# A decoder layer with expert retrieval: one more top-k in the dense stage, gate rows by a matmul with ones, one-hots shared with VectorE

## The chip, the cores and the metric

One NeuronCore of a Trainium2 chip runs the whole kernel. Its engines are TensorE (PE in the rows), VectorE (DVE), ScalarE (ACT), GpSimd (POOL) and SyncE (SP, which here only issues transfers). The metric is the time on the device in microseconds, the median of three runs. A second measurement, one profiled execution, gives the rows below.

## The reference, cut to what matters

One layer on 1024 tokens of width 1024. Six modulation rows come from the condition c: two shifts, two scales, two gates. After the mixing part (a gMLP half and an S5 state space half, joined by an output projection with gate gt1), a PEER block retrieves for each token and each of 8 heads the 16 best of 16,384 experts, and adds their weighted sum with gate gt2.

```python
cond = jax.nn.silu(c)
mod = cond @ w_ada[l] + b_ada[l]
sh1, sc1, gt1, sh2, sc2, gt2 = jnp.split(mod[:, None, :], N_MOD, axis=-1)
h = _rmsnorm(x, g_mix[l]) * (1.0 + sc1) + sh1
z = h @ w_in[l]                     # gMLP u, gMLP v, S5 input
y = jnp.concatenate([y_gm, y_ssm], axis=-1) @ w_out[l]
x = x + gt1 * y
h2 = _rmsnorm(x, g_ffn[l]) * (1.0 + sc2) + sh2
x = x + gt2 * _peer(h2, w_q[l], peer_keys[l], peer_u[l], peer_v[l])
return _rmsnorm(x, g_final)

# _peer, for a block t of 128 tokens
s = jnp.einsum('thcd,hckd->thck', q, keys)
top_s, top_i = lax.top_k(s, PEER_TOPK)
best_s, pos = lax.top_k(cand_s, PEER_TOPK)      # of all 16 x 16 sums
g = jax.nn.softmax(best_s, axis=-1)
act = jax.nn.gelu(jnp.einsum('thkd,td->thk', u_tab[idx], t))
return jnp.einsum('thk,thkd->td', g * act, v_tab[idx])
```

## The kernel before

The 1024 tokens are eight blocks of 128. A dense stage does the mixing part for all blocks, in two halves of four, and then for each block b an output projection (outproj, tiles po, with the gate row bc), a score (score, item sb: transposes ptf, queries pq, scores psc on TensorE) and a top-k on VectorE (route, item r, in 28 steps; tiles m, ixs, scr, mk).

The experts of blocks 0 to 4 are then computed for all 16,384 experts in 128 tiles of 128, weighted by a matrix G that is zero where an expert wasn't chosen. G is built by scatter (item s): for each of a token's 128 choices one-hot rows are compared out (hot and a on VectorE), scaled by the weight (b, on VectorE for every dv[block]-th pair of choices and on ScalarE for the rest), and multiplied on TensorE (pgs), copied out (GS) and written to HBM (G_d). An expert tile i has stage1 (pa: 192 matmuls with u, in three products of split values), a weighing (w, wh, wl), and per four tiles a stage2 (res and pd, with v). u and v of a tile are split by ScalarE and VectorE after their load. Five lead tiles go first, as the item ld.

The experts of blocks 5 to 7 are fetched row by row with indirect transfers from GpSimd: per block 128 rows of u (ru, multiplied on VectorE, summed on ScalarE), then 128 rows of v (rv, accumulated into gacc on VectorE). This is the generator side_work. It first does the top-k of the blocks from NDB + early on, here block 7 alone, then releases the score's buffers, then fetches; the loop over expert tiles pulls per steps of it for each tile, 6.3 here. Each block's end is finish: scale by gt2, add, normalise (msf, rf), scale by g_final, write.

The order of the dense stage is written by a table, CFG["plan"]: each item has a start and a duration, and needs other items; its steps are sorted by these times and become the program. A scheduler then orders each engine's instructions from there. So a changed entry moves whole items on all engines.

The modulation parts enter in two forms. As columns (mod_late): the sum of the weighted rows of w_ada, mc, is made on VectorE and summed over partitions by eight matmuls of 128 x 1 (pm), and b_ada is added on VectorE. The two gates are wanted as rows on all partitions: row_bcast makes eight diagonal tiles (diag) on VectorE and multiplies each by ones (pb_gt1, pb_gt2), then ScalarE copies the result (bc). gate1 does this for gt1, late_gt2 for gt2, which is written to HBM (gt2_d). mod5 makes mc5 from eight row blocks of w_ada, two in each load (wada5), with two buffers.

Of the kernel before, what the change touches and what calls it, by code (L numbers as in the profile page):

```python
# [41 lines left out]
CFG = dict(xo=[2, 3, 4, 0, 1], gt=3, ss=7, hs=2, b1=6, nw=6, raw=1, ngb=3, rows=4, lead=5, per=6.3, dv=[6, 9, 9, 2, 99], early=2,  # L42
# [6 lines left out]
    gt=(858.2, 122), rel=(739, 334), s4=(981.8, 131.5), r5=(916.4, 58.6), r6=(989.9, 124.6), ld=(776, 675.7),  # L49
# [6 lines left out]
    wo1=(-962.7, 7.3), so=(-926.7, 23.4), vn=(-891, 2.4), g1=(-703.9, 14.2), ax=(-882.1, 8.1), m3=(-856.1, 38.5),  # L56
# [41 lines left out]
def tile_hybrid_layer(ctx: ExitStack, tc: tile.TileContext, a, out, cfg=CFG):  # L98
# [27 lines left out]
    def bankB(name):  # L126
        return psB.tile([P, 2, 512], F32, tag="b", name=name)
# [83 lines left out]
    def mod_sums(i):  # L211
        mp = bankB(f"mp{i}").rearrange("p a b -> p (a b)")
        k = 0
        for w, n in early[i]:
            for kk in range(n):
                if k:
                    V.scalar_tensor_tensor(mp, w[:, kk], cs[:, k:k + 1], mp, op0=ALU.mult, op1=ALU.add)
                else:
                    V.tensor_scalar(mp, w[:, kk], cs[:, k:k + 1], None, op0=ALU.mult)
                k += 1  # L220
            yield
        mc = sm.tile([P, D], F32, tag="x", name=f"mc{i}", bufs=3)
        A.copy(mc, mp)
        mod_late(i, mc)

    def mod_load(i, src):
        ws, k = [], 0
        for c in src:
            n = {"X": 4, "p": 2, "x": 1}[c]
            v = a["w_ada"][k * P:(k + n) * P, i * D:(i + 1) * D].rearrange("(k p) n -> p k n", p=P)  # L230
            if c == "X":
                w = sB.tile([P, 4, D], F32, tag="X", name=f"wada{i}_{k}", bufs=1)
            elif c == "x":
                w = sm.tile([P, 1, D], F32, tag="x", name=f"wada{i}_{k}", bufs=3)
# [815 lines left out]
    def mod5():  # L1050
        mc = sm.tile([P, D], F32, tag="x", name="mc5", bufs=3)
        for k in range(0, KD, 2):
# [19 lines left out]
    def prep_steps(n):  # L1072
# [13 lines left out]
        au=(lambda: z_u(0, wzu[0]), 4, "wu"), ax=(lambda: mix(0), 2, "au vn"), g1=(gate1, 1, "m2"),  # L1086
# [3 lines left out]
        gt=(gt2_row, 1, "m5"), rel=(release, NDB, "gt op7 sb7"), ld=(lambda: lead(0, L), 2 * L, "rel"))  # L1090
# [402 lines left out]
```

## Time and profile before

| | us |
|---|---|
| median of three runs | 2656.88 (2655.66 to 2659.79) |
| the profiled execution | 2655.86 |
| its span | 2653.9 |
| dense stage up to the first tile after the five lead tiles | about 918 |
| expert tiles 5 to 127 | to about 2600 |

In the rows a matmul's count x is of passes: a float32 matmul is two of them. A bracket at the end of a row is the engine's idle time before it, with the line of what ended it. The granted clock is 1.00 at 2.4 GHz. VectorE is busy 85% of the span, ScalarE 49%, GpSimd 44%.

### The profile page before, as it was taken

The numbers are of one execution on the slowest core, as the hardware profiler recorded it, in microseconds if no ns is written. First come the engines' busy times: TensorE is split into PE (matmuls) and PEld (weight loads), VectorE is DVE, ScalarE is ACT, GpSimd is POOL, SyncE is SP. The second block draws the span as 40 slices with busy tenths as digits, with TensorE's granted clock in tenths as the row PEclk, the third lists the DMA queues.
The fourth block names the chain that finished last, engine by engine and source line by source line (L and its number), as shares of the span: only waits on it lengthen the run. The fifth ranks groups of instructions, "written<-read, shape, count | busy, mean of one in ns | idle before, by whom it ended". The sixth has DMA issues, their size and how long they took to land. (4 is left out here: it accounts for less than half of the span.)

```text
span 2653.9 us, 39049 instructions
## 1 busy us (share of the span) xinstructions
PE 2538.1 (96%) x14119; PEld 2168.1 (82%) x14119; DVE 2267.8 (85%) x4215; ACT 1312.8 (49%) x2315; POOL 1180.9 (44%) x842
## 2 busy tenths in 40 slices
PE   6999999999877999999999999999999999999997
PEld 2548677678666898989999989999999988999986
DVE  7984699869899888789989888889999888899898
ACT  2311246568868377773222577762223767732222
POOL 0001000000000177676667578766665767776660
PEclk9996999999988999999999999999999999999999
DMA  9546233444636699999999999899998999999993
GB/s 362 108 121 217 101 122 104 126 136 135 181 118 193 218 328 326 343 327 364 341 340 375 325 336 330 331 354 364 341 355 326 334 345 343 325 368 345 343 365 139
DMA packets 301761, 726.85 MB, mean 274 GB/s; under 512 B 42448, under 2 KB 133072, under 8 KB 301152
## 3 DMA queue, kind: packets, MB, share of 16 engines
q0 software_dynamic: 112832, 411.09, 42.4%
q1 hardware_dynamic: 165600, 254.48, 28.6%
q10 hardware_dynamic: 23136, 58.79, 6.2%
q8 instruction: 111, 1.82, 0.3%
q14 instruction: 82, 0.67, 0.1%
HBM read 660.70 MB, written 62.39 MB: 272 GB/s over the span
## 5 line engine op out<-in xcount | busy, mean ns | idle before, releaser
L888 POOL DMA_INDIRECT ru<-in_peer_u_dram,ix x384 | 637.7, 1661 | 897.6 <-issue 745.1
L959 PE MATMUL pa<-Th,u 128*128 128x320 f32 x4096 | 911.3, 310 | 4.9 <-DVE u L936 3.1
L959 PEld LDWEIGHTS pa<-Th,u 128*128 128x128 f32 x4096 | 688.4, 188 | 8.7 <-DVE u L936 3.6
L888 POOL DMA_INDIRECT rv<-in_peer_v_dram,ix x384 | 522.8, 1361 | 257.4 <-DVE gacc L916 168.0
L959 PE MATMUL pa<-Tl,u 128*128 128x320 f32 x2048 | 633.4, 309 | 0.0
L899 DVE TENSOR_TENSOR ru<-ru,hn 128x2048 f32<-128x2048 f32 x192 | 438.6, 2289 | 113.1 <-DMA ru<-in_peer_u_dram,ix 106.6
L894 ACT ACTIVATE jk<-ru 128x1024 bf16<-128x1024 f32 x384 | 405.4, 1056 | 213.2 <-issue 167.7
L916 DVE SCALAR_TENSOR_TENSOR gacc<-rv,act,gacc 128x1024 f32<-128x1024 f32 x381 | 489.2, 1284 | 6.4 <-DVE u L936 0.4
L1006 PE MATMUL pd<-v,wh 128*128 128x512 f32 x1280 | 402.6, 390 | 3.2 <-ACT wh L980 1.6
L997 PE MATMUL res<-v,wh 128*128 128x512 f32 x1280 | 400.7, 390 | 0.8 <-ACT wh L980 0.8
L959 PEld LDWEIGHTS pa<-Tl,u 128*128 128x128 f32 x2048 | 385.3, 188 | 1.7
L1006 PEld LDWEIGHTS pd<-v,wh 128*128 128x128 f32 x1280 | 238.8, 188 | 52.5 <-ACT wh L980 2.5
L997 PEld LDWEIGHTS res<-v,wh 128*128 128x128 f32 x1280 | 239.6, 188 | 50.4 <-ACT wh L980 1.6
L961 ACT ACTIVATE w<-pa 128x320 f32<-128x320 f32 x256 | 108.7, 431 | 333.7 <-PE pa L959 311.9
L698 ACT ACTIVATE b<-hot,gT 128x128 f32<-128x128 f16 x520 | 233.5, 537 | 61.0 <-PE pgs L700 36.0
L1006 PE MATMUL pd<-v,wl 128*128 128x512 f32 x640 | 248.7, 390 | 1.7 <-DVE wl L982 1.6
L997 PE MATMUL res<-v,wl 128*128 128x512 f32 x640 | 248.1, 389 | 1.3 <-DVE wl L982 1.3
L935 ACT CAST u<-ur 128x1024 fp32r<-128x1024 f32 x128 | 133.5, 1043 | 205.3 <-DMA ur<-in_peer_ut_dram 79.0
L700 PE MATMUL pgs<-a,b 128*128 128x128 f32 x1280 | 188.9, 299 | 46.2 <-DVE a L690 19.3
L700 PEld LDWEIGHTS pgs<-a,b 128*128 128x128 f32 x1280 | 169.9, 207 | 68.4 <-ACT b L698 35.3
L936 DVE TENSOR_TENSOR u<-ur,u 128x1024 fp32r<-128x1024 f32 x128 | 156.3, 1221 | 29.7 <-ACT u L935 23.2
L943 ACT CAST v<-vr 128x1024 fp32r<-128x1024 f32 x128 | 133.7, 1045 | 94.1 <-DMA vr<-in_peer_v_dram 76.8
(349 smaller groups left out, 3050.4 us busy)
## 6 DMA issues: line engine op xcount, KB each, us to landing
vr<-in_peer_v_dram SPq DMA_DIRECT2D x128, 512.0 KB
ur<-in_peer_ut_dram SPq DMA_DIRECT2D x128, 512.0 KB
G_d<-GS SPq DMA_DIRECT2D x40, 1024.0 KB
Gt<-G_d ACTq DMA_DIRECT2D x64, 640.0 KB
wada<-in_w_ada_dram SPq DMA_DIRECT2D x17, 1024.0 KB
wo<-in_w_out_dram SPq DMA_DIRECT2D x8, 1024.0 KB
ru<-in_peer_u_dram,ix POOLq DMA_INDIRECT x384
rv<-in_peer_v_dram,ix POOLq DMA_INDIRECT x384
```

The source lines that it names most:

```text
L698: A.activation(b1[:, n], hot[:, :, o + n], AF.Copy, scale=gT[:, s1 + o + n:s1 + o + n + 1])
L700: T.matmul(pg[:, o // 4, (o % 4) * P:(o % 4 + 1) * P], b1[:, o % 2], a1[:, o % 4], start=True, stop=True)
L888: G.indirect_dma_start(out=row[:, e], out_offset=None, in_=a[src], in_offset=bass.IndirectOffsetOnAxis(ap=ix[:, s0 + e:s0 + e + 1], axis=0))
L894: A.activation(junk, row[:, e], AF.Copy, accum_out=act[:, s + e:s + e + 1])
L899: V.tensor_mul(row, row, bcast(hn, 1, GP))
L916: V.scalar_tensor_tensor(ac, row[:, e], w, ac, op0=ALU.mult, op1=ALU.add)
L935: A.copy(u[:, 0], ur)
L936: V.tensor_tensor(u[:, 1], ur, u[:, 0].bitcast(F32), op=ALU.subtract)
L943: A.copy(v[:, 0], vr)
L959: T.matmul(pa[:, :NN], l[:, k, :], r[:, k, ns], start=(k == 0 and m == 0), stop=(k == KD - 1 and m == 2))
L997: T.matmul(res[tb][n], l[:, ts], r[:, n * 512:(n + 1) * 512], start=(g == 0 and q == 0 and m == 0), stop=(g == NGR - 1 and q == QG - 1 and ...
L1006: T.matmul(po, l[:, ts], r[:, n * 512:(n + 1) * 512], start=(q == 0 and m == 0), stop=(q == QG - 1 and m == 2))
```

## The change

Some numbers of the table and a new helper:

- early goes from 2 to 1: block 6's top-k leaves the plan (item r6) and is done in side_work, ahead of block 7's. per goes from 6.3 to 6.6.
- dv of block 4 goes from 99 to 2: half of its b pairs are made on VectorE, where ScalarE made all but one.
- The items rel and ld get shorter durations (rel 60 instead of 334, ld 150 instead of 675.7), and rel needs m5 instead of gt.
- gate_row takes the place of row_bcast and mod_late for the mods 2 and 5: a row of b_ada (br, 1024 elements, reordered in the transfer) is loaded by SyncE, and four matmuls of 512 columns with ones sum mc over partitions and add br into a row on all partitions (pb), which ScalarE copies. gt1 is made in mod_sums(2), gt2 in mod5; items g1 and gt are gone.

```diff
-CFG = dict(..., per=6.3, dv=[6, 9, 9, 2, 99], early=2,
+CFG = dict(..., per=6.6, dv=[6, 9, 9, 2, 2], early=1,
...
-    gt=(858.2, 122), rel=(739, 334), s4=(981.8, 131.5), r5=(916.4, 58.6), r6=(989.9, 124.6), ld=(776, 675.7),
+    rel=(739, 60), s4=(981.8, 131.5), r5=(916.4, 58.6), ld=(776, 150),
...
         mc = sm.tile([P, D], F32, tag="x", name=f"mc{i}", bufs=3)
         A.copy(mc, mp)
-        mod_late(i, mc)
+        if i == 2:
+            gt1 = sm.tile([P, D], F32, name="bc1", bufs=1)
+            gate_row(i, mc, gt1)
+        else:
+            mod_late(i, mc)
...
+    def gate_row(i, mc, dst):
+        br = sm.tile([P, D], F32, tag="x", name=f"br{i}", bufs=3)
+        nc.sync.dma_start(br[:1].rearrange("o (k p) -> o k p", p=P), a["b_ada"][:, i * KD:(i + 1) * KD].rearrange("p (o k) -> o k p", o=1))
+        pb = bankB(f"pb{i}")
+        for n in range(2):
+            for r, p in ((mc, P), (br, 1)):
+                T.matmul(pb[:, n], ones[:p], r[:p, n * 512:(n + 1) * 512], start=(p == P), stop=(p == 1))
+        A.copy(dst, pb.rearrange("p a b -> p (a b)"))
...
-    def row_bcast(dst, col, name):
-        pb = bankB(f"pb_{name}")
-        for k in range(KD):
-            dg = sm.tile([P, P], F32, tag="diag", name=f"diag_{name}{k}", bufs=2)
-            V.tensor_scalar(dg, ident, col[:, k:k + 1], None, op0=ALU.mult)
-            T.matmul(pb[:, k // 4, (k % 4) * P:(k % 4 + 1) * P], ones, dg, start=True, stop=True)
-        A.copy(dst, pb.rearrange("p a b -> p (a b)"))
-        return dst
...
             if k == KD - 2:
-                mod_late(5, mc)
-            yield
-
-    def gt2_row():
-        late_gt2()
-        yield
+                bc2 = sm.tile([P, D], F32, tag="x", name="bc2", bufs=3)
+                gate_row(5, mc, bc2)
+                nc.scalar.dma_start(gt2_d, bc2)
+            yield
...
-        gt=(gt2_row, 1, "m5"), rel=(release, NDB, "gt op7 sb7"), ld=(lambda: lead(0, L), 2 * L, "rel"))
+        rel=(release, NDB, "m5 op7 sb7"), ld=(lambda: lead(0, L), 2 * L, "rel"))
```

TensorE's order around pzu of the first half, the matmuls that stand ahead of py (pzv and pzu are gMLP projections), before:

```order
L491 MATMUL pzv0_3_1100<-wzv_0_305,hT0_0_129 128x512 x4
L491 MATMUL pzv0_3_1100<-wzv_1_306,hT0_1_130 128x512 x4
L248 MATMUL pm2_1113<-ones_80,mc2_1111 128x1 x8
L536 MATMUL pzu0_0_1464<-hT0_0_129,wzu_0_1123 128x512 x4
L536 MATMUL pzu0_0_1464<-hT0_1_130,wzu_1_1124 128x512 x4
```

and now:

```order
L505 MATMUL pzv0_3_1100<-wzv_0_305,hT0_0_129 128x512 x4
L505 MATMUL pzv0_3_1100<-wzv_1_306,hT0_1_130 128x512 x4
L256 MATMUL pb2_1116<-mc2_1111,ones_80 128x512
L256 MATMUL pb2_1116<-br2_1114,ones_80 128x512
L256 MATMUL pb2_1116<-mc2_1111,ones_80 128x512
L256 MATMUL pb2_1116<-br2_1114,ones_80 128x512
L550 MATMUL pzu0_0_1463<-hT0_0_129,wzu_0_1122 128x512 x4
L550 MATMUL pzu0_0_1463<-hT0_1_130,wzu_1_1123 128x512 x4
```

The eight matmuls pm2 of one column give way to four of 512 columns, pb2, at the same place.

TensorE's order from the GLU matmuls pg of the first half to the first score (ptf0), before; po0 and po1 are output projections of blocks 0 and 1, pb_gt1 a piece of gate row 1, pm5 the columns of mod 5:

```order
L637 MATMUL po0_1916<-wo2_1814,ss0_1823 128x512 x4
L637 MATMUL po0_1916<-wo3_1812,ss0_1823 128x512 x4
L557 MATMUL pb_gt1_1857<-diag_gt17_1879,ones_80 128x128
L637 MATMUL po1_2043<-wo0_809,gm0_1463 128x512 x4
L637 MATMUL po1_2043<-wo1_1506,gm0_1463 128x512 x4
L637 MATMUL po1_2043<-wo2_1814,ss0_1823 128x512 x4
L637 MATMUL po1_2043<-wo3_1812,ss0_1823 128x512
L248 MATMUL pm5_1900<-ones_80,mc5_1883 128x1 x8
L726 MATMUL ptf0_0_1955<-ident_75,xn0_1952 128x128 x4
L726 MATMUL ptf0_1_1964<-ident_75,xn0_1952 128x128 x4
L637 MATMUL po1_2043<-wo3_1812,ss0_1823 128x512 x3
```

and now, from the end of pg:

```order
L617 MATMUL pg0_3_1847<-ysT0_1817,wg0_1815 128x512
L256 MATMUL pb5_1875<-mc5_1855,ones_80 128x512
L256 MATMUL pb5_1875<-br5_1873,ones_80 128x512
L256 MATMUL pb5_1875<-mc5_1855,ones_80 128x512
L256 MATMUL pb5_1875<-br5_1873,ones_80 128x512
L637 MATMUL po0_1888<-wo0_809,gm0_1462 128x512 x4
L637 MATMUL po0_1888<-wo1_1505,gm0_1462 128x512 x4
L637 MATMUL po0_1888<-wo2_1813,ss0_1822 128x512 x4
L637 MATMUL po0_1888<-wo3_1811,ss0_1822 128x512 x4
L637 MATMUL po1_2015<-wo0_809,gm0_1462 128x512 x4
L637 MATMUL po1_2015<-wo1_1505,gm0_1462 128x512 x4
L637 MATMUL po1_2015<-wo2_1813,ss0_1822 128x512 x4
```

The work on mod 5 stood behind most of po1; it now stands ahead of po0 and needs all of mc5 in its first row.

VectorE's order near the end, before; gacc2 is the sum of block 7, fin2 the rows gt2 and g_final, v and wl belong to the last expert tiles, xf2 is block 7's output:

```order
L846 TENSOR_TENSOR gacc2_19251<-gacc2_19251,fin2_21552 128x1024
L944 TENSOR_TENSOR v125_21841<-vr125_21839,v125_21841 128x1024
L847 TENSOR_TENSOR xf2_21555<-xf2_21555,gacc2_19251 128x1024
L982 TENSOR_TENSOR wl62_21837<-w124_21579,wh62_21835 128x1280
L141 TENSOR_SCALAR msf7_21557<-msf7_21557 128x1
L133 TENSOR_SCALAR rsq_i_21565<-msf7_21557 128x1
L978 TENSOR_TENSOR w126_21844<-w126_21844,Gt31_0_21637 128x2x320
L134 TENSOR_SCALAR rf7_21563<-rsq_i_21565 128x1
L136 TENSOR_TENSOR rsq_t_21564<-rf7_21563 128x1
```

and now, from the last but two rows of gacc2 on; acc are dense sums, res the last products of TensorE:

```order
L912 SCALAR_TENSOR_TENSOR gacc2_18830<-rv2_124_20991,act2_16462,gacc2_18830 128x1024
L940 TENSOR_TENSOR v127_21875<-vr127_21873,v127_21875 128x1024
L912 SCALAR_TENSOR_TENSOR gacc2_18830<-rv2_124_20991,act2_16462,gacc2_18830 128x1024
L1031 TENSOR_TENSOR acc_6425<-acc_6425,fin2_21069 128x512
L912 SCALAR_TENSOR_TENSOR gacc2_18830<-rv2_126_21064,act2_16462,gacc2_18830 128x1024
L1031 TENSOR_TENSOR acc_6425<-acc_6425,fin2_21069 128x1024 x2
L912 SCALAR_TENSOR_TENSOR gacc2_18830<-rv2_126_21064,act2_16462,gacc2_18830 128x1024
L842 TENSOR_TENSOR res0_7477<-res0_7477,fin2_21069 128x512
L1032 TENSOR_TENSOR x1_1_21879<-x1_1_21879,acc_6425 128x512
L842 TENSOR_TENSOR res1_7478<-res1_7478,fin2_21069 128x512
L842 TENSOR_TENSOR gacc2_18830<-gacc2_18830,fin2_21069 128x1024
L842 TENSOR_TENSOR res2_7479<-res2_7479,fin2_21069 128x512
```

The scaling and adding of block 7's sum stood among the last v and w rows; it now stands behind the first res row.

## Rows read from the trace of the kernel before

**Rows 1.** The page: engine, busy us, share of the span, instructions.
```profile
PE 2538.1 (96%) x14119; PEld 2168.1 (82%) x14119; DVE 2267.8 (85%) x4215; ACT 1312.8 (49%) x2315; POOL 1180.9 (44%) x842
```

**Rows 2.** Windows: length, busy (x) of PE, PEld, DVE, ACT, POOL; clock, DMA, GB/s.
```profile
199.00:244.00 45.00, 45.00 (x195) 41.63 (x194) 21.55 (x50) 4.78 (x8) 1.43 (x2) 0.51 0.52 157
...
262.00:300.00 38.00, 36.90 (x144) 21.05 (x143) 22.98 (x41) 8.97 (x17) 0.00 (x0) 1.00 0.49 169
300.00:720.00 420.00, 397.06 (x2471) 305.94 (x2470) 368.18 (x1504) 280.39 (x620) 0.00 (x0) 0.99 0.41 124
...
760.00:860.00 100.00, 75.91 (x510) 70.49 (x510) 92.59 (x405) 83.62 (x180) 0.00 (x0) 0.87 0.57 169
...
918.00:1210.00 292.00, 286.72 (x1610) 260.16 (x1609) 235.76 (x162) 206.96 (x348) 216.98 (x131) 1.00 0.91 331
...
1475.00:2600.00 1125.00, 1123.49 (x6330) 1027.25 (x6329) 981.81 (x803) 558.56 (x883) 771.63 (x513) 1.00 0.93 342
```

**Rows 3.** TensorE's timeline, 160 to 218: start, us, engine, line, operation [idle before].
```profile
165.21 1.84 PE L248 MATMUL pm<-ones,mc 128*128 128x1 f32 x16
166.91 27.71 PE L536 MATMUL pzu<-hT,wzu 128*128 128x512 f32 x64
194.46 1.05 PE L572 MATMUL py<-U,TOE 128*128 128x128 f32 x8
...
198.43 2.54 PE L578 MATMUL py<-X,CN 64*128 64x128 f32 x14 [2.49 <-DVE X L477]
200.90 2.07 PE L572 MATMUL py<-U,TOE 128*128 128x128 f32 x8
```

**Rows 4.** TensorE's timeline, 236 to 300.
```profile
237.18 3.78 PE L578 MATMUL py<-X,CN 64*128 64x128 f32 x16
...
248.05 3.68 PE L617 MATMUL pg<-ysT,wg 128*128 128x512 f32 x8
...
260.82 7.03 PE L617 MATMUL pg<-ysT,wg 128*128 128x512 f32 x16
...
278.20 7.13 PE L637 MATMUL po<-wo,gm 128*128 128x512 f32 x16 [1.10 <-ACT bc L558]
...
294.65 5.52 PE L736 MATMUL pq<-tq,wq 128*128 128x128 f32 x48
```

**Rows 5.** VectorE's timeline, 218 to 300.
```profile
218.70 2.49 DVE L510 TENSOR_TENSOR vn<-vn,cst 128x512 f32<-128x512 f32 x4
243.00 0.69 DVE L546 TENSOR_TENSOR mx<-pmx,cst 128x512 f32<-128x512 f32 x1 [21.81 <-PE pmx L544]
...
266.89 1.09 DVE L621 TENSOR_TENSOR ss<-ysT,sg 128x512 f32<-128x512 f32 x1 [0.62 <-ACT sg L620]
...
276.09 2.61 DVE L1057 SCALAR_TENSOR_TENSOR mc<-wada,cs,mc 128x1024 f32<-128x1024 f32 x2 [2.58 <-DMA wada<-in_w_ada_dram]
...
281.20 1.27 DVE L1057 SCALAR_TENSOR_TENSOR mc<-wada,cs,mc 128x1024 f32<-128x1024 f32 x1
```

**Rows 6.** VectorE's groups by line, 600 to 720: count, busy us, mean ns, idle before.
```profile
L694 DVE TENSOR_TENSOR b<-hot,gT 128x256 f32<-128x256 f16 x39 | 23.4, 609 | 1.5 <-PE pgs L700 1.3
```

**Rows 7.** ScalarE's groups by line, 755 to 857.
```profile
L698 ACT ACTIVATE b<-hot,gT 128x128 f32<-128x128 f16 x126 | 55.0, 519 | 7.7 <-DVE hot L685 7.7
```

**Rows 8.** TensorE's timeline, 722 to 772.
```profile
741.04 1.25 PE L557 MATMUL pb_gt<-diag_gt,ones 128*128 128x128 f32 x4 [7.28 <-DVE diag_gt L556]
...
765.03 1.04 PE L726 MATMUL ptf<-ident,xn 128*128 128x128 f32 x8
```

**Rows 9.** VectorE's timeline, 2590 to 2654.
```profile
2602.41 1.22 DVE L846 TENSOR_TENSOR gacc<-gacc,fin 128x1024 f32<-128x1024 f32 x1
...
2613.40 1.28 DVE L855 SCALAR_TENSOR_TENSOR xf<-xf,rf,fin 128x1024 f32<-128x1024 f32 x1
...
2617.17 2.96 DVE L1036 TENSOR_TENSOR x<-x,acc 128x512 f32<-128x512 f32 x3
2625.18 0.70 DVE L846 TENSOR_TENSOR res<-res,fin 128x512 f32<-128x512 f32 x1 [5.04 <-PE res L997]
```

More of the change, by code (lines that the diff above doesn't have):

```diff
@@ L41 @@
 FMAX = 3.0e38
-CFG = dict(xo=[2, 3, 4, 0, 1], gt=3, ss=7, hs=2, b1=6, nw=6, raw=1, ngb=3, rows=4, lead=5, per=6.3, dv=[6, 9, 9, 2, 99], early=2,
+CFG = dict(xo=[2, 3, 4, 0, 1], gt=3, ss=7, hs=2, b1=6, nw=6, raw=1, ngb=3, rows=4, lead=5, per=6.6, dv=[6, 9, 9, 2, 2], early=1,
            hp=600, eo=(2, 4), em={2: 'pppxx', 4: 'Xpp'}, seg=4, plan=dict(
@@ L55 @@
     sc=(-1112.1, 4.9), wq0=(-1115, 14.4), wq1=(-1142.8, 77.1), au=(-1181.6, 1.4), wo0=(-1165.4, 1),
-    wo1=(-962.7, 7.3), so=(-926.7, 23.4), vn=(-891, 2.4), g1=(-703.9, 14.2), ax=(-882.1, 8.1), m3=(-856.1, 38.5),
+    wo1=(-962.7, 7.3), so=(-926.7, 23.4), vn=(-891, 2.4), ax=(-882.1, 8.1), m3=(-856.1, 38.5),
     ag=(-741.7, 2.7), mid=(-803.3, 8.8), wo2=(-878.1, 13.4), wo3=(-805.6, 6.4), wq2=(-441.9, 1.1),
@@ L211, in mod_sums @@
     def mod_sums(i):
+        nonlocal gt1
         mp = bankB(f"mp{i}").rearrange("p a b -> p (a b)")
@@ L599, in load_wo @@
         nc.sync.dma_start(wo[i], a["w_out"][i * 256:(i + 1) * 256, :].rearrange("(k p) n -> p k n", p=P))
-    def gate1():
-        nonlocal gt1
-        gt1 = row_bcast(sm.tile([P, D], F32, name="bc1", bufs=1), mod[2], "gt1")
-        yield
     def glu(hf, slot):
@@ L652, in outproj @@
         yield
-    def late_gt2():
-        bc2 = sm.tile([P, D], F32, tag="x", name="bc2", bufs=3)
-        nc.scalar.dma_start(gt2_d, row_bcast(bc2, mod[5], "gt2"))
     gx = kp = sC = tk = iot = iot8 = None
@@ L1085, in tile_hybrid_layer @@
         cst=(lambda: one(load_cst), 1, "z0"), wu=(lambda: one(load_wzu), 1, "z0"),
-        au=(lambda: z_u(0, wzu[0]), 4, "wu"), ax=(lambda: mix(0), 2, "au vn"), g1=(gate1, 1, "m2"),
+        au=(lambda: z_u(0, wzu[0]), 4, "wu"), ax=(lambda: mix(0), 2, "au vn"),
         ag=(lambda: glu(0, slotA), 4, "so"), mid=(mid, 1, "so m2 m4 m3"), m5=(mod5, 4, "mid sc"),
@@ L1096, in tile_hybrid_layer @@
         items[f"oa{b}"] = lambda b=b: outproj(b), 1, "zu" if h1 else "ax wo0 wo1"
-        items[f"op{b}"] = f"oa{b}", 1, f"oa{b} " + ("gl" if h1 else "g1 ag wo2 wo3")
+        items[f"op{b}"] = f"oa{b}", 1, f"oa{b} " + ("gl" if h1 else "m2 ag wo2 wo3")
         items[f"sb{b}"] = lambda b=b: score(b), NSC, f"op{b} wq3 ky m3 m4 mid"
```

## The prediction

> **What bounds the kernel now.** First the page's busy times and the windows by stage. TensorE is busy 96% of the span [rows 1], and in the expert stage nearly without a gap: 286.72 of 292 us in 918 to 1210, 1123.49 of 1125 in 1475 to 2600 [rows 2]. There are 128 expert tiles and the chain of work runs on TensorE through them, so that stage's length is fixed. The time therefore follows three things: when the stage starts, what TensorE loses in it, and what follows it. Between 300 and 720 TensorE is busy 397 of 420 us and VectorE 368 [rows 2]: a shift that arrives at 300 is handed on nearly whole. Before 300 TensorE is also the chain, but at half clock for a while: in 199 to 244 it is busy all 45 us at a granted clock of 0.51, that is 1.2 instead of 2.4 GHz [rows 2]. In 760 to 860, the scatter of block 4, VectorE is the fuller one, 92.59 of 100 against TensorE's 75.91 [rows 2]. At the end VectorE finishes alone. So the change has four places: 195 to 295 (gate rows), 718 to 857 (scatter without a top-k), the expert stage (two top-k in side work), the tail.
>
> **Gate rows, the clock.** The trace shows the scan's last step arriving late: TensorE starts pzu at 166.91, reaches the first matmuls on the scan's states, and then waits 2.49 us until 198.43 [rows 3]. Eight TOE passes take 1.05 us before that wait and 2.07 after it [rows 3], so the clock fell on it, and it stayed low to the end of py, whose last passes start at 237.18 [rows 4]; 262 to 300 shows 1.00 again [rows 2]. The new gate row of mod 2 puts four float32 matmuls of 512 columns, eight passes, where eight matmuls of one column stood. Passes of that form take 7.03 us for 16 [rows 4], 0.44 each, so 3.5 us in place of 1.84 [rows 3]; pzu starts 1.75 us later and the wait shrinks to about 0.7 us, since the scan on VectorE is not touched. Does the clock still fall? The nearest row on one side is the 1.10 us wait ahead of 278.20, in a window that kept 1.00 [rows 4, 2]; on the other the 2.49 itself. 0.7 lies on the near side, so I take it that the clock stays. Then py, which lasts from 194.46 to 237.18 + 3.78 = 240.96 [rows 3, 4], takes half as long for all passes behind the wait: it ends near 220. VectorE has vn ready at 221.2 (218.70 + 2.49) and then sits idle for 21.81 us until pmx [rows 5]; that idle time goes, pmx starts at 221.2 and pg, after pmx and pm3 as before (248.05 − 240.96, 7.1 us, and 0.1 between them), at 228.4 instead of 248.05 [rows 4]. The Trainium skill (TensorE: Matmul & The Clock Gate, Part 1, What's actually happening) says that the gate follows how busy the array has been and that its phase differs from run to run. By that rule 0.7 us of waiting may also fall badly; here the trace has only the two waits, and the case in which the clock falls is a rival below.
>
> **Gate rows, the new wait.** This gain is spent again. In the new order pb5, the gate row of mod 5, stands on TensorE directly behind pg and ahead of all of po0 and po1. Its operand mc5 is a chain on VectorE: eight steps of 1.28 us, the last starting at 281.20 [rows 5]. Before, that chain ran beside po0 and po1, which cover it (pg's last 16 passes start at 260.82 and take 7.03, so it ends at 267.7; po0, po1 and what lies between them fill the time to pq at 294.65 [rows 4]). The chain can't start sooner in the new order: it is still behind three of the ss rows (266.89 is the third), and its second half waits for weights (2.58 us at 276.09 [rows 5]) whose transfer is issued when its first tiles are read. From pg's end to mc5's end is 281.20 + 1.27 − 267.7 = 14.8 before; one row of 1.23 that evicts po0 lies ahead of the last step there and is behind it in the new order, which leaves 13.5. The row of b_ada, 1024 elements of four bytes fetched singly, is queued on SyncE ahead of those weights. Nothing like it is in the trace: at 0 it costs nothing, at the top as much as the wait for a weight tile, 2.58; nearer to 0, as 4 KB stand against 1024 KB, so I take 0.5. So TensorE waits 14 us. That is far over 2.49, so the clock falls here: pb5 takes 7 us instead of 3.5 and about 1.5 more is lost in po0. From pg's start: pg 14.1 (32 passes of 0.44), wait 14, pb5 7, po0 14.1 + 1.5, po1 14.1, and 3.5 until pq (ptf and the copy behind it): 228.4 + 68.3 = 296.7. Before it is 294.65 [rows 4]. **First term: +2.1 us**, bounds −1 (the wait is 12 and the clock recovers within pb5) and +6 (b_ada at 2.58, loads not yet there). If the clock falls as before, pg starts at 248.05 + 1.75 and the term is 249.8 + 68.3 − 294.65 = +23.5.
>
> **Scatter of block 4.** Removed from VectorE: block 6's top-k and the eight diag rows of gate row 5 (of which TensorE awaited one for 7.28 us [rows 8]). Added: half of block 4's 64 b rows, which ScalarE made as 128 small ones of 519 ns [rows 7]; on VectorE a pair is 609 ns [rows 6], 0.53 from one start to the next. Walking VectorE's order from block 5's first top-k row to the last a row of block 4, and giving each row its duration of the groups, I get 121.5 us before and 107.7 after (top-k rows −28.5, other rows −2.2, b rows +16.9): 13.8 less. On ScalarE about 62 b fall away, 62 × 0.42 = 26 us, so it isn't the limit. But block 7's score moves: xn7 stands after 54.3 us of that stretch instead of 38.3, and TensorE has put the score in one piece between the first 32 and the remaining pgs matmuls of block 4, where before only 12 stood ahead of it. ptf starts at 765.03 now [rows 8]; it would start near 780 and last 20 us (its matmuls: 14.3 pq, 3.6 psc, 1.8 others). The eleventh a row waits for pgs behind it, since there are two a buffers, and VectorE has no top-k left to fill that time with: it loses some 10 us of the 13.8. **Second term: −4 us**, bounds −9 (half the stall) and +1 (all of it and the clock of this stretch, 0.87 [rows 2], lower still).
>
> **Expert stage.** What remains of block 6's top-k, and block 7's, are pulled between tiles 0 and 10. VectorE's order has 101.6 us of rows from the last a to the first product with a gathered row, 58.2 before; the rows up to wl1 and v3, for which stage 2 of the first group waits, grow only from 36.3 to 38.2 and from 46.2 to 47.9. VectorE has 56 us spare in 918 to 1210 alone [rows 2]. So the first tiles lose about 2 us, later ones perhaps 1. **Third term: +3 us**, bounds −3 (the earlier lead tiles start sooner) and +10 (gathers that are issued faster, at 6.6 steps a tile, take VectorE ahead of u and v rows).
>
> **Tail.** The gathers start some three tiles later and VectorE's order gives them some 40 tiles a block as before, so they end later: the last gacc rows now stand behind the last v row, and behind the first res row come gacc's scaling (1.22), the three sums into x (2.96), the sum into xf (about 1.22), ten small rows of 0.1 and xf's last scaling (1.28) [rows 9]. Before all these ran ahead of the wait of 5.04 us for res [rows 9], that is, free. From the first res row to the end the order has 33.1 us of rows instead of 25.3. **Fourth term: +7.5 us**, bounds +4 (a part fits into waits for msf) and +8.
>
> **Sum.** +2.1 − 4 + 3 + 7.5 = +8.6 us on the profiled run's 2655.86; that run lies 1.0 below the median of 2656.88, so about 2665. Its own range, the bounds not all at one end, is 2654 to 2677. A measurement of this kernel can tell about 0.2%, 5.3 us, from no change.
>
> **Rivals.**
> Clock falls (slower by more). The remaining 0.7 us is enough, and py runs at 1.2 GHz as now. For it: in py TensorE was busy throughout and the clock still did not rise for 45 us [rows 2], so py's passes don't hold it up well. Against it: 300 to 720 kept 0.99 with many short matmuls and waits among them [rows 2]. First term +23.5 instead of +2.1: 2655.9 + 30 + 1 = 2687.
> Freed VectorE time counts in full (faster). The top-k that is taken out was in VectorE's way all over 718 to 918, and no wait takes its place; VectorE then leads, and the gathers too, by what it gains. For it: 92.59 of 100 us busy in 760 to 860 [rows 2]. Against it: the order above. It gives −13.8 in the scatter and nothing in the tail: 2.1 − 13.8 + 3 = −8.7, so 2648. It decides where VectorE waits less than 3 us for pgs in that stretch and the last gacc stands before the end of the last res.
> Nothing moves. The top-k is only pushed from one place where VectorE has no time to another, and gate rows are hidden in both: 2657.
>
> **How the numbers follow.** Forecast (clock stays, long wait at pb5, tail grows) 0.50; clock falls 0.18; freed time in full 0.25; nothing moves 0.07. Within the forecast (2665, own range 2654 to 2677) I put 0.04 faster, 0.33 same, 0.63 slower; in the faster rival 0.75 faster and 0.25 same; the clock's fall is slower. Faster: 0.02 + 0.19 = 0.21; same: 0.165 + 0.0625 + 0.07 = 0.30; slower 0.49. The range 2646 to 2690 reaches to both rivals and leaves out about half of the faster one and a third of the other, some 0.19.
>
> **What would show it.** In the new profile: the granted clock in 199 to 244, and py's end near 220; a TensorE wait of about 14 us for mc5 ahead of the matmuls of line 256, followed by a stretch at half clock; pq of block 0 within 5 us of 294.65; VectorE waiting over 10 us for pgs in block 4's scatter; pa's first matmul of tile 5 within 5 us of where it is; TensorE's loss in the expert stage within 10 us of now; and xf and x rows after the first res row in the tail, with no wait of 5 us ahead of it. The forecast fails if the clock falls at py all the same, if pb5 doesn't wait, or if the gathers catch up and the tail stays as it is.

## The result and the profile after

The changed kernel takes 2693.37 us (median of 4 runs, 2686.86 to 2698.72) against 2656.27 for the kernel before: 1.0142 times as long, 95% interval 1.0118 to 1.0167. It is slower by some 37 us, 28 more than forecast, and lies just outside the range. Its profiled execution took 2686.86, 6.5 below its median, with a span of 2684.8; the accounts below are of that execution, and cover the 30.9 us by which its span is longer.

The windows of the profile after, same stretches and columns as [rows 2] (length, busy of PE, PEld, DVE, ACT, POOL, clock, DMA share, GB/s):

```profile
199.00:244.00 45.00, 37.42 (x250) 30.49 (x249) 26.21 (x57) 6.06 (x9) 8.63 (x52) 0.93 0.94 285
244.00:262.00 18.00, 8.27 (x15) 3.21 (x13) 8.17 (x8) 2.75 (x4) 0.00 (x0) 0.69 0.58 175
262.00:300.00 38.00, 31.88 (x57) 12.45 (x58) 10.24 (x19) 2.16 (x3) 0.00 (x0) 0.73 0.22 78
300.00:720.00 420.00, 398.77 (x2488) 304.76 (x2486) 362.30 (x1491) 271.42 (x599) 0.00 (x0) 1.00 0.40 123
...
760.00:860.00 100.00, 77.47 (x513) 71.83 (x514) 83.07 (x263) 62.34 (x127) 0.00 (x0) 0.85 0.53 160
...
918.00:1210.00 292.00, 287.66 (x1597) 260.82 (x1596) 242.06 (x319) 189.11 (x310) 178.71 (x111) 0.99 0.83 298
...
1475.00:2600.00 1125.00, 1118.81 (x6282) 1020.45 (x6281) 977.80 (x800) 557.26 (x880) 762.34 (x513) 1.00 0.93 343
```

The clock is nearly whole in 199 to 244 (0.93 instead of 0.51), and what falls behind it is new: TensorE is busy 8 of 18 us in 244 to 262 and the clock is 0.69 and 0.73 up to 300. From 300 to 720 little has changed, and VectorE has 10 us less to do in 760 to 860. TensorE's timeline (start, us, instruction, idle time before it), which answers to [rows 3] and [rows 4]:

```profile
166.01 1.02 PE L256 MATMUL pb<-mc,ones 128*128 128x512 f32 x2
...
170.12 27.73 PE L550 MATMUL pzu<-hT,wzu 128*128 128x512 f32 x64
...
220.18 2.05 PE L583 MATMUL py<-X,CN 64*128 64x128 f32 x16
...
227.53 7.11 PE L617 MATMUL pg<-ysT,wg 128*128 128x512 f32 x16
242.23 10.04 PE L617 MATMUL pg<-ysT,wg 128*128 128x512 f32 x16 [7.58 <-DMA ysT<-ys_d]
268.12 2.08 PE L256 MATMUL pb<-mc,ones 128*128 128x512 f32 x2 [15.85 <-DVE mc L1053]
...
276.13 10.16 PE L637 MATMUL po<-wo,gm 128*128 128x512 f32 x16
286.13 7.03 PE L637 MATMUL po<-wo,ss 128*128 128x512 f32 x16
...
307.88 14.56 PE L732 MATMUL pq<-tq,wq 128*128 128x128 f32 x128
```

The gate row of mod 2 takes four times 1.02 to 1.12 us, pzu (170.12) starts 3.2 us later, the scan's states arrive without a wait, and the passes on them take 2.05 us for 16, where they took 3.78 [rows 4]. So pg starts at 227.53, 20.5 sooner. But there are two holes: 7.58 us in the middle of pg, waiting for ysT (the output ys of the S5 half, written to HBM and loaded back), and 15.85 us ahead of pb, waiting for mc. Each pair of passes of pb takes 2.07 to 2.08 us, about twice what such a pair took at 166: half clock. Before, pieces of po stood between the pieces of pg:

```profile
251.79 4.46 PE L637 MATMUL po<-wo,gm 128*128 128x512 f32 x10
256.08 3.60 PE L617 MATMUL pg<-ysT,wg 128*128 128x512 f32 x8
```

Where the time goes is read from the same points of both traces:

| point in the trace | before | after | difference | change in the step |
|---|---|---|---|---|
| pg starts | 248.1 | 227.5 | −20.5 | −20.5 |
| block 0's queries start | 294.7 | 307.9 | +13.2 | +33.7 |
| block 7's output projection ends | 733.3 | 745.7 | +12.4 | −0.8 |
| last a row of block 4's scatter ends | 854.6 | 859.5 | +4.9 | −7.5 |
| lead tile 4 ends | 889.7 | 894.6 | +4.9 | 0 |
| tile 5 starts | 918.2 | 930.1 | +11.9 | +7.0 |
| tile 125 starts | 2590.2 | 2607.2 | +17.0 | +5.1 |
| end of the span | 2653.9 | 2684.8 | +30.9 | +13.9 |

The first gathered product starts at 976.2 instead of 921.9, the first accumulation of block 7 at 2387.9 instead of 2338.4: some 50 us late from first to last.

### The profile page after: what moved, and what is told of

Its sections match the earlier page's. It is cut to its first block, busy times and chain, and to the rows that moved or that the text cites. A ratio compares the mean times of both kernels' runs of the same rounds, so it can differ in the third digit from the quotient of the medians.

```text
span 2684.8 us, 38941 instructions
## 1 busy us (share of the span) xinstructions
PE 2532.5 (94%) x14071; PEld 2146.8 (80%) x14071; DVE 2276.1 (85%) x4228; ACT 1290.2 (48%) x2255; POOL 1166.3 (43%) x842
## 5 line engine op out<-in xcount | busy, mean ns | idle before, releaser
L884 POOL DMA_INDIRECT ru<-in_peer_u_dram,ix x384 | 621.8, 1619 | 976.4 <-issue 819.2
L694 ACT ACTIVATE b<-hot,gT 128x128 f32<-128x128 f16 x458 | 207.9, 548 | 57.2 <-PE pgs L696 37.5
L940 DVE TENSOR_TENSOR v<-vr,v 128x1024 fp32r<-128x1024 f32 x128 | 156.2, 1220 | 17.3 <-ACT v L939 16.0
```

The source lines that it names most:

```text
L694: A.activation(b1[:, n], hot[:, :, o + n], AF.Copy, scale=gT[:, s1 + o + n:s1 + o + n + 1])
L884: G.indirect_dma_start(out=row[:, e], out_offset=None, in_=a[src], in_offset=bass.IndirectOffsetOnAxis(ap=ix[:, s0 + e:s0 + e + 1], axis=0))
L940: V.tensor_tensor(v[:, 1], vr, v[:, 0].bitcast(F32), op=ALU.subtract)
```

## The experiments

Each label's kernel differs from the one that its text names by the edit shown. Spans and points in time are of one profiled execution of each kernel, medians of all its runs; a ratio is to the kernel before on the same chip in the same session, while differences between two changed kernels are of medians from different sessions.

**Gate rows.** One part undone and one part alone:

```diff
 # gate5_old, from the changed kernel; row_bcast, late_gt2, gt2_row and the plan's gt as before
-                gate_row(5, mc, bc2)
+                mod_late(5, mc)
...
-        rel=(release, NDB, "m5 op7 sb7")
+        gt=(gt2_row, 1, "m5"), rel=(release, NDB, "gt op7 sb7")
```

> The changed kernel with the gate row of mod 5 made the old way (columns behind the first output projections, diagonal tiles at 733 to 757), all else as changed. Theory (the wait for mod 5's row behind pg, 15.85 us, and the uncovered wait for ysT, 7.58 us, cost what the kept clock gained): pg starts near 227.5 as in the changed kernel, po0 and po1 fill both waits, and the first pq comes at 275 to 280 instead of 307.9, so some 28 to 33 us come off there; the old row's diagonal tiles cost 3 to 8 back near 745; total 2662 to 2670. Rival (the wait only hides transfers that are late anyway): pq comes near 300 and the total stays above 2680.

```diff
 # gate2_only, from the kernel before; gate1 and its item go
-        mod_late(i, mc)
+        if i == 2:
+            gt1 = sm.tile([P, D], F32, name="bc1", bufs=1)
+            gate_row(i, mc, gt1)
+        else:
+            mod_late(i, mc)
```

> The kernel before with nothing changed but the gate row of mod 2 made by four matmuls with ones. Theory (the shorter wait ahead of the scan's states keeps TensorE's clock at 1.00 through py): granted clock about 1.00 in 199 to 222, first pq 15 to 20 us before 294.65, total 2637 to 2643. Rival (the clock's stay was luck of that one execution, or a later wait takes it back): clock near 0.5 in 199 to 244 or first pq within 3 us of 294.65, total 2652 to 2660.

gate5_old: 2645.99 us, 0.9948 of the time before (0.9931 to 0.9965), 16 below what was expected at the least. The first queries start at 277.5, as the theory had it. TensorE's timeline shows how: pieces of po stand between the pieces of pg again, and from pg to the queries there is only one wait, 3.91 us for xn.

```profile
228.78 1.96 PE L626 MATMUL pg<-ysT,wg 128*128 128x512 f32 x4
...
240.02 4.46 PE L646 MATMUL po<-wo,gm 128*128 128x512 f32 x10
244.31 3.60 PE L626 MATMUL pg<-ysT,wg 128*128 128x512 f32 x8
...
256.33 13.90 PE L646 MATMUL po<-wo,ss 128*128 128x512 f32 x32
...
275.81 1.94 PE L735 MATMUL ptf<-ident,xn 128*128 128x128 f32 x8 [3.91 <-DVE xn L660]
277.55 4.70 PE L745 MATMUL pq<-tq,wq 128*128 128x128 f32 x34
```

The rest of the gain was not expected: the scatter ends at 811.7, 43 us sooner than before, while block 7's output projection is only 17.4 sooner. So the new gate row of mod 5 costs 30.3 us (277.55 against 307.88) at its place, and another 18 in the scatter, whose order is another without the old row; at the end the two kernels are 46.4 apart.

gate2_only: 2632.09 us, 0.9892 (0.9853 to 0.9931). The clock is 1.00 from 196 to 262, the first queries start at 278.2, 16.5 sooner than before, and this reaches the end: the span is 2634.1, 19.8 shorter. This kernel beats both. Its window from 199 to 222, with the columns as above:

```profile
199.00:222.00 23.00, 23.00 (x183) 21.27 (x182) 19.82 (x46) 4.18 (x7) 1.43 (x2) 1.00 0.81 256
```

Is it the clock, or the diagonal tiles that go? An added load on TensorE tells:

```diff
 # clock_fill, from the kernel before; nobody reads the bank
         mod_late(i, mc)
+        if i == 2:
+            pf = bankB("fill")
+            for n in range(4):
+                T.matmul(pf[:, n % 2], ones, mc[:, n % 2 * 512:(n % 2 + 1) * 512], start=True, stop=True)
```

> The kernel before with four matmuls of 512 columns added behind pm2, into a bank that nobody reads; gate row 1 stays as it was, diagonal tiles and all. Theory (only TensorE's shorter wait ahead of the scan's states counts): the wait of 2.49 us shrinks below 1, granted clock about 1.00 in 199 to 222, first pq 12 to 18 us before 294.65, total 2636 to 2645 although TensorE has more to do. Rival (the gain of gate2_only came from the eight diagonal tiles and matmuls that it takes out between pmx and po0): first pq 2 to 5 us later than before, total 2656 to 2662.

Measured: 2637.72 us, 0.9938 (0.9906 to 0.9971), first queries at 278.0, 16.6 sooner than before. More work for TensorE makes the kernel 19 us faster by the medians (its profiled execution, at 2644.63 slower than that median, has a span only 11.2 shorter than before):

```profile
168.47 1.84 PE L252 MATMUL pm<-ones,mc 128*128 128x1 f32 x16
170.18 3.68 PE L228 MATMUL fill<-mc,ones 128*128 128x512 f32 x8
173.69 27.63 PE L540 MATMUL pzu<-hT,wzu 128*128 128x512 f32 x64
201.16 1.05 PE L576 MATMUL py<-U,TOE 128*128 128x128 f32 x8
202.15 2.05 PE L582 MATMUL py<-X,CN 64*128 64x128 f32 x16
```

pzu starts 6.8 us later than before, of which 3.5 are the fill; the rest is a shift that both engines have in this execution, as VectorE makes the last of the awaited states 3.0 later too (201.4 against 198.4). No wait is left ahead of the states (202.15 follows 201.16 without one), and these passes run at full clock. So filling the wait is enough, and the rival falls.

The kernel before does not lose this time in every execution. In the sessions of these experiments ten of its 85 further executions took 2630.55 to 2644.72 us at a mean granted clock of 0.980 to 0.988, the time of a kernel with the wait filled; the others took 2649.97 or more at 0.978 or less. topk_only below, which keeps the wait, does the same: three of ten took 2655.30 to 2658.27 at 0.981 to 0.983, the others 2671.31 or more at 0.972 to 0.977. The kept traces of both kernels are of executions that lose the time, and show the wait (2.49 and 2.51 us) with the half clock behind it. No trace of a quicker one was kept, so it is open whether the wait was shorter there or the clock outlived it.

The row of mod 5, kept but placed behind block 1's projection:

```diff
 # gate5_late, from the changed kernel
-    m5=(-490.1, 3.4)
+    m5=(165, 3.4)
```

> The changed kernel with the new gate row of mod 5 kept, but its item planned behind block 1's output projection (start 165 instead of -490), so that its four matmuls follow block 0's queries. Theory (what cost is the place of the row ahead of po0, not the row itself): no wait of over 3 us ahead of the matmuls of the gate row, first pq at 275 to 282 instead of 307.9, total 28 to 36 us below the changed kernel: 2652 to 2665. Rival (the row itself costs: its chain on VectorE or the transfer of 1024 single elements): first pq or the end of block 0's scores stays 10 us or more above the old row's 277.5 and 297.1, total above 2670.

Measured: 2661.86 us, 1.0034 (1.001 to 1.0057), 31 below the changed kernel, so the place is the larger part. The queries start at 276.8. But the row is not free there either:

```profile
276.75 15.32 PE L732 MATMUL pq<-tq,wq 128*128 128x128 f32 x128
294.89 1.40 PE L256 MATMUL pb<-mc,ones 128*128 128x512 f32 x2 [2.82 <-DVE mc L1053]
...
300.22 2.07 PE L256 MATMUL pb<-br,ones 1*128 1x512 f32 x2
302.22 3.09 PE L743 MATMUL psc<-keys,tq 64*128 64x128 f32 x16
```

pb still waits 2.82 us for mc, runs at half clock again (2.07 for two passes), and block 0's scores end at 309.8 instead of 297.1 in gate5_old. Each theory held for a part: 31.1 us at the queries were the place, 12.7 at the scores the row. The scatter stays as in the changed kernel (last a row 8.3 us gained against block 7's projection, not 25.5).

The hole in pg:

```diff
 # wo_behind, from the changed kernel
-    wo2=(-878.1, 13.4), wo3=(-805.6, 6.4)
+    wo2=(-690, 5), wo3=(-680, 5)
```

> The changed kernel with the loads of wo2 and wo3 planned later (-690 and -680), by which SyncE issues one of the two megabytes behind the second ysT load instead of ahead of it. Theory (TensorE's 7.58 us wait for ysT in the middle of pg is this load in the queue behind two weight loads): the wait is 2 to 5 us, the first pq 3 to 6 us sooner than 307.9, total 2684 to 2692. Rival (the wait is the way of ys through HBM, which is as long in any order): 6.5 to 8.5 us, first pq within 2 us of 307.9.

```profile
226.38 7.11 PE L617 MATMUL pg<-ysT,wg 128*128 128x512 f32 x16
239.17 9.32 PE L617 MATMUL pg<-ysT,wg 128*128 128x512 f32 x16 [5.68 <-DMA ysT<-ys_d]
264.48 2.07 PE L256 MATMUL pb<-mc,ones 128*128 128x512 f32 x2 [15.99 <-DVE mc L1053]
```

The wait is 5.68: between the two expectations. With the old order of the loads four profiled kernels show 7.49 to 8.08 us (changed kernel, after_per, score_first, topk_back), so the load moved behind ysT is worth some 2 us. What the rest is (the other load, one of wq, or the way of ys through HBM) was not tried. Total 2686.52; the queries start at 303.8, 4.1 sooner, of which 1.1 comes from an earlier pg.

**Scatter of block 4.** Half of the b rows on VectorE, taken out where the top-k is gone, and added where it is not:

```diff
 # g5old_dv, from gate5_old
-    dv=[6, 9, 9, 2, 2]
+    dv=[6, 9, 9, 2, 99]
 # g2_dv, from gate2_only
-    dv=[6, 9, 9, 2, 99]
+    dv=[6, 9, 9, 2, 2]
```

> The kernel gate5_old with block 4's b rows back on ScalarE (dv 99). Theory (with the top-k gone ScalarE's b rows are what the scatter waits for): TensorE waits for b on ScalarE over 10 us in block 4's scatter, the last a row comes 10 to 16 us later than in gate5_old (811.7), tile 5 6 to 12 us later, total 2650 to 2658. Rival (VectorE remains the bound, b rows on it cost): the last a row comes sooner and the total is 2640 or less.

> The kernel gate2_only with half of block 4's b rows on VectorE and nothing else (top-k of block 6 still in the dense stage). Theory (with the top-k there VectorE is the fuller engine in the scatter): last a row 0 to 8 us later than in gate2_only (844.0), TensorE waits for b on VectorE, total 2632 to 2642. Rival (ScalarE's b rows bound it, as without the top-k): last a row 8 us or more sooner, total 2620 to 2628.

g5old_dv took 2648.19 us (span 2646.1 against 2638.4), its last a row ended at 824.3 instead of 811.7, tile 5 started 9.6 us later. TensorE waited for ScalarE's b for 7.0 us, less than expected, and the total is below the theory's and above the rival's. The larger wait is VectorE's, whose a rows wait for pgs to free their buffers (line waited for, us in total, times, longest us):

```profile
DVE a L699 <- PE pgs L709: 23.3, 19, 6.7
```

g2_dv took 2648.72 us, 17 more than gate2_only, and more than either expectation. Its last a row ends 3.1 us later, tile 5 starts 6.7 later, and TensorE waits for VectorE's b:

```profile
PE pgs L709 <- DVE b L703: 14.4, 8, 4.6
PE pgs L709 <- DVE a L699: 13.0, 11, 3.4
```

So the split shortens the scatter where the top-k has left VectorE (by 12.6 us) and lengthens it where it has not. In the total it costs 17 us there, while the gain of 2 us here is not clear of noise. The other 11 us of g2_dv arise behind tile 5 (tile 125 is 17.3 later than in gate2_only); why was not settled.

The wait of VectorE behind block 7's score, which the prediction had named, is in the changed kernel:

```profile
DVE b L690 <- PE pgs L696: 13.3, 2, 13.1
```

It is 13.1 us in one piece, where "some 10" were forecast, though on a b row and not on the eleventh a row. Its cause was tried by moving the score ahead of the scatter:

```diff
 # score_first, from the changed kernel
-    op7=(897.9, 60.4)
+    op7=(897.9, 15)
```

> The changed kernel with one number of the plan changed (op7's duration 15 instead of 60.4), by which block 7's score stands ahead of block 4's scatter on TensorE and not between its 32nd and 33rd matmul. Theory (VectorE's b and a rows stand 13 us behind that score): no wait of VectorE for pgs over 4 us, the last a row of block 4 at 845 to 852 instead of 859.5, tile 5 6 to 12 us sooner than 930.1, total 6 to 15 below the changed kernel's 2693: 2678 to 2687. Rival (the wait only moves, VectorE has the same rows to do): last a row within 4 us of 859.5, total 2688 to 2698.

Measured: 2697.8 us, last a row at 865.8. The theory falls: now TensorE waits at the score's first instruction, with the scatter's matmuls behind it, and VectorE waits as long as before.

```profile
PE ptf L722 <- DVE xn L651: 15.0, 1, 15.0
```

```profile
DVE b L690 <- PE pgs L696: 17.7, 3, 14.7
```

What is late is xn7 on VectorE. In the changed kernel the small rows that make its scale are strung out among b, a and top-k rows, from 757.9 to 788; in gate5_old from 726.8 to 747.1. xn7 in the two:

```profile
788.35 0.78 DVE L651 TENSOR_SCALAR xn<-x,r 128x1024 f32<-128x1024 f32 x1
```

```profile
747.13 0.75 DVE L660 TENSOR_SCALAR xn<-x,r 128x1024 f32<-128x1024 f32 x1
```

Behind the end of block 7's output projection that is 42.6 and 31.2 us. Neither place of the score on TensorE mends that; an earlier xn7 was not tried.

**Top-k and gathers.** Moved alone, and moved back in two kernels:

```diff
 # topk_only, from the kernel before
-early=2
+early=1
-    r6=(989.9, 124.6),
 # topk_back, from the changed kernel, and g5old_topk, from gate5_old
-early=1
+early=2
+    r6=(989.9, 124.6),
```

> The kernel before with block 6's top-k moved into the side work and nothing else. Theory: the scatter of block 4 ends 5 to 15 us sooner, the gathers start 40 us later, and expert stage and tail lose 15 to 25: total 2662 to 2672. Rival (the freed VectorE time counts in full, the loss is due to the other parts): the tail stays as before and the total is 2640 to 2652.

> The changed kernel with block 6's top-k back in the dense stage (early=2, its old entry in the table), all else as changed. Theory (the gathers that start 50 us later cost the wait in the first stage 2, 5 us in the expert stage and 14 us in the tail): first product with a gathered row 920 to 935 instead of 976, the last gathered row before the last v, and the tail as before; 20 to 26 us come off, 5 to 10 come back in the scatter: 2672 to 2682. Rival (the tail is late because 6.6 steps a tile and b rows on VectorE fill it, not because of the start): the tail still ends 10 us or more later behind tile 125 than before, and the total is above 2685.

> The kernel gate5_old with block 6's top-k back in the dense stage, so the gate row of mod 2, the half of the b rows and the short lead entries remain. Theory (the later start of the gathers costs more in the expert stage and the tail than the top-k costs in the scatter): tile 5 starts 8 to 14 us later than in gate5_old (893.6), the first gathered product 20 us or more sooner, the tail 12 shorter; total 2627 to 2638. Rival (with gate rows mended the freed VectorE time is worth more than the late gathers): 2646 or more.

topk_only: 2671.76 us, 1.0039 (1.0008 to 1.0071), span 2673.3. The scatter ends 13.3 us sooner than before, but lead tile 4 only 0.7 sooner, tile 5 starts 4.6 later, tile 125 11.1 later and the span ends 19.4 later: the theory's account, in its size. (The ratio amounts to some 10 us only, in part because three of its ten executions are the quicker ones named above.) topk_back: 2676.11 us, 17 below the changed kernel. Its scatter is 17.4 us longer, its gathers start at 949.9 (15 later than expected), tile 125 comes no later behind tile 5 than before, and the end follows tile 125 by 64 us as before (77.6 in the changed kernel). g5old_topk: 2643.25 us, 3 below gate5_old and not clearly different: there the top-k in the dense stage costs 34 us in the scatter, of which 11.4 are left at tile 5 and 15.0 at tile 125, and 11.9 come back in the tail. These parts are as the theory had them, the total is between the two expectations: with the old gate row 5 the two nearly cancel.

Is it the gathers' end that makes the tail long? A kernel with less to gather:

```diff
 # short_gather, from gate5_old: leaves out the last 12 of block 7's 128 experts
+            ns = NS - 12 if n == NGB - 1 else NS
-            for s in range(0, NS, GP):
+            for s in range(0, ns, GP):
```

> The kernel gate5_old with the last 12 of block 7's 128 gathered experts left out, in both products. At 1680 us for 384 such experts this takes 50 us off the gathers' end and nothing off anything else. Theory (the gathers take as long as the expert stage has, so each start 50 us later ends in the tail): tile 125 within 4 us of gate5_old, the wait for res on VectorE back at 4 to 6 us, the end 9 to 14 us sooner behind tile 125: total 2631 to 2638. Rival (the tail is long by the order of the last rows, whatever the gathers' end): end behind tile 125 as in gate5_old, total 2643 to 2649.

Measured: 2628.65 us, 0.9909 (0.9881 to 0.9937). Tile 125 starts at 2563.5 (gate5_old 2562.5), and the span ends 11.7 us sooner. VectorE again waits for res, as in [rows 9], while in gate5_old TensorE waited for rows of ScalarE and VectorE (the first line is short_gather, the other two are gate5_old):

```profile
2597.28 0.70 DVE L855 TENSOR_TENSOR res<-res,fin 128x512 f32<-128x512 f32 x1 [8.37 <-PE res L1007]
```

```profile
PE res L1006 <- ACT v L952: 4.4, 1, 4.4
PE pd L1015 <- DVE x L856: 3.9, 1, 3.9
```

The tail follows the gathers' end. All the profiled kernels agree: where the last gacc row ends less than 11 us behind the start of tile 125, the tail from there lasts 63.2 to 64.5 us; where it ends 24.4 us behind, 67.9; where it ends 35 to 45 behind, 72.0 to 78.6. Before, the gathers go from 921.9 to 2597.8, nearly the whole expert stage, which ends with res at 2629: some 30 us to spare, and some 50 late, in a stage that is itself 17 late, is too much.

**Two numbers of the plan alone.**

```diff
 # after_per, from the changed kernel
-per=6.6
+per=6.3
 # g2_leads, from gate2_only
-    rel=(739, 334), ... ld=(776, 675.7)
+    rel=(739, 60), ... ld=(776, 150)
```

> The changed kernel with 6.3 instead of 6.6 side steps a tile. Theory (the gathers go at the rate of their transfers and of VectorE, not at that number): first and last gathered rows within 6 us of the changed kernel, total 2688 to 2699. Rival (6.6 crowds VectorE in the expert stage): tile 125 is 4 us or more closer to tile 5, total 2680 to 2687.

> The kernel gate2_only with the shorter entries for rel and ld and nothing else. Theory (the lead tiles placed among the scatter only order rows that the data decide anyway): tile 5 within 3 us of gate2_only's 905.5, total 2628 to 2637. Rival (they pay, as g5old_topk's tile 5 came no later than gate2_only's although half of the b rows stood on VectorE): tile 5 5 us or more sooner, total 2620 to 2627.

after_per: 2689.16 us, gathers 3 to 7 us later all along, tile 125 78.6 us from the end (77.6): the number does nothing that these runs can tell. g2_leads: tile 5 2 us sooner, span 2632.5 against 2634.1, but a median of 2639.85 against 2632.09: no gain shown either.

## Why the prediction was wrong

**Clock (held, by another size).** The clock stayed at 1.00 in py, as forecast, but the wait of 0.7 us, from which this was argued, was not there. The eight passes of pb2 started 0.8 later than pm2 had (166.01 against 165.21) and took 4.1 us where the sum had 3.5; pzu started 3.2 later, not 1.75, and the states arrived without a wait. What a wait of 0.7 would have done no run shows. The rival in which the clock falls did not come. gate2_only and clock_fill show the mechanism alone: first queries 16.5 and 16.6 us sooner, medians 26 and 19 lower. The Trainium skill (TensorE: Matmul & The Clock Gate, Part 1, What's actually happening) says that the gate's phase differs from run to run. All profiled kernels with a filled wait show 1.00 from 199 to 222; the ten quicker executions of the kernel before would fit that remark, but without a trace of one they do not show it.

**First term (+2.1, measured +13.2).** The step that failed is "pg 14.1 (32 passes of 0.44)". It took 24.7 from 227.53 to 252.3: 7.58 waiting for ysT and 3 at half clock after that wait. Before, pieces of po stood between the pieces of pg (251.79 is one) and covered the way of ysT. The prediction moved po behind pb5 and did not ask what it had covered within pg; it looked only at the cover for mc5. That alone is 10.6 of the 11.1 missing. The other sizes were near: wait 15.85 for 14, pb 8.0 for 7, po0 16.9 for 15.6, and 1.2 instead of 3.5 up to the queries.

**Second term (−4, measured −7.5).** Within its bounds; the wait behind the score was there with 13.1 us. Its cause was told as a later xn7, the score's place and the two a buffers; score_first shows that the place does not decide, as the wait stays when the score is moved, and that TensorE then waits for xn7.

**Third term (+3, measured +12.1).** 7.0 of it are in the first stage 2, "about 2 us" in the prediction. TensorE waits there for v:

```profile
PE pd L1002 <- DVE v L940: 4.7, 2, 3.7
PE pd L1002 <- ACT v L939: 1.0, 1, 1.0
```

The failed step is "the first tiles lose about 2 us". The rows up to v3 were counted (47.9 against 46.2), as if the v rows had only to follow each other; but tile by tile they stand behind top-k rows, and lead tiles that end at 894.6 want them. The longest of these waits ends with the v row at 907.76, behind a top-k row (mk):

```profile
906.63 1.22 DVE L1417 TENSOR_TENSOR mk<-po,tk_st 128x2048 int16<-128x2048 int16 x1
907.76 1.22 DVE L940 TENSOR_TENSOR v<-vr,v 128x1024 fp32r<-128x1024 f32 x1
```

The waits sum to 5.7 of the 7.0. That the moved top-k brings them the experiments bear out: from the end of lead tile 4 to tile 5 the kernels with early=2 take 28.2 to 30.0 us, those with early=1 33.8 to 35.6 (score_first 54.4, for another wait). The counting also left out that VectorE, ahead of these rows, stood idle for 8.40 us up to 878.90, where a top-k row waited for scores from HBM; such waits in that stretch were at most 2.0 before. The remaining 5.1 came between tiles 5 and 125, where 1 was forecast; waits for wl on VectorE, 6.6 us up to 2560 against 2.9 before, are the largest there. This part is no clear difference: the profiled kernels with early=2 take 1665.3 to 1675.9 us from tile 5 to tile 125, the kernel before 1672.1 and the changed one 1677.1.

**Fourth term (+7.5, measured +13.9).** The failed step is "bounds ... and +8": only the rows behind the first res row were added, and those ahead of it put at nothing. VectorE's timeline at the end, which answers to [rows 9]:

```profile
2620.73 3.96 DVE L912 SCALAR_TENSOR_TENSOR gacc<-rv,act,gacc 128x1024 f32<-128x1024 f32 x3
...
2634.81 7.88 DVE L912 SCALAR_TENSOR_TENSOR gacc<-rv,act,gacc 128x1024 f32<-128x1024 f32 x6
2642.61 1.22 DVE L940 TENSOR_TENSOR v<-vr,v 128x1024 fp32r<-128x1024 f32 x1
...
2649.01 1.28 DVE L912 SCALAR_TENSOR_TENSOR gacc<-rv,act,gacc 128x1024 f32<-128x1024 f32 x1
2650.21 0.69 DVE L842 TENSOR_TENSOR res<-res,fin 128x512 f32<-128x512 f32 x1
...
2652.01 1.22 DVE L842 TENSOR_TENSOR gacc<-gacc,fin 128x1024 f32<-128x1024 f32 x1
...
2668.68 1.27 DVE L851 SCALAR_TENSOR_TENSOR xf<-xf,rf,fin 128x1024 f32<-128x1024 f32 x1
```

VectorE has hardly a gap left: six gacc rows (7.88 us) stand ahead of the last v row, which is done 26.6 us later than before, while the products of tile 127 with u end only 16.5 late. TensorE's last res product ends 22.0 late, and the pd behind it waits for VectorE once more, so TensorE ends 29.4 late:

```profile
PE pd L1002 <- DVE x L843: 7.9, 1, 7.9
```

The first res row at 2650.21 has no wait of 5 us ahead of it, as forecast, and the gacc and xf scalings follow, as forecast: direction and place held. From the first res row to the end it takes 34.6 us instead of 28.7, 5.9 more where the sum had 7.5. But the first res row itself comes 43.0 us behind the start of tile 125 instead of 35.0, and these 8.0 were in no term: the rows from the last v row on were counted as covered by the 5.04 us of [rows 9] (7.7 us of them against 4.1), and those ahead of the v row not at all. short_gather shows that these 12 to 14 us go with the gathers' end.

**Rivals.** "Freed VectorE time counts in full" did not come in this kernel. gate5_old, with the same top-k and b rows but the old gate row 5, gains 25.5 us in the scatter (−42.9 against −17.4), so its mechanism exists in the scatter. But it did not count in full there either: at tile 5 only 7.2 of the 25.5 us are left against the projection's end, 12.3 go in the tail, and the gain of 0.5% that gate5_old has is less than what gate2_only has from the clock alone (1.1%). What the changed kernel lost in the scatter is taken here to be the order around block 7's score; no run mended that order alone.

Summed: 13.2 − 0.8 − 7.5 + 7.0 + 5.1 + 13.9 = 30.9. The gate row of mod 5 at its place is the largest loss, the late gathers the second, and the clock's gain, 20.5 us at the start of pg, is inside the first number.

## What to carry to other kernels

When an instruction that waits is moved ahead of others on an in-order engine, ask for each of those others what it had covered so far: here po covered two waits, and only one was priced. A step taken out of the front and put ahead of a chain that fills the whole next stage (here 1676 us of gathers with some 30 to spare) comes out again at the end. And where a short wait of TensorE is followed by a long stretch at half clock, it is worth filling, with useful work or useless: 3.7 us of matmuls that nobody reads lowered the median by 19.

## What the runs showed of the hardware

In the traces of the kernel before and of topk_only TensorE's clock fell after one wait (2.49 and 2.51 us), and in the first it stayed at 1.2 GHz (0.51 granted) for 45 us though TensorE was busy throughout. With that wait gone the same passes ran at 2.4 GHz to their end, 2.05 us for 16 instead of 3.78. In ten of 85 further executions the kernel before had the time of one without the loss. Behind the two longer waits of the changed kernel, where pg, pb and po followed, the clock came back sooner: the 16 passes behind the 7.58 us wait took 10.04 us where 16 take 7.03, some 6 us at half clock; behind the 15.85 us wait pb's eight passes (8.0 us) and a part of the next 16 (10.16 us) were slow, some 14 us. The row of 1024 single elements of b_ada was never what was waited for: its matmuls follow those of mc without a gap (267 to 277 in the changed kernel).
